# A two-group encoder layer: adaLN by channel quarters in column tiles, branch B's inverse rms through DRAM, the residual gate in the first head

## The chip, the cores and the metric

The kernel runs on one core of a Trainium2 chip. The metric is the time of one launch on the device, in microseconds. A NeuronCore has TensorE (PE: matmuls and transposes; PEld is its weight load), VectorE (DVE), ScalarE (ACT), GpSimd (POOL) and SyncE (SP). In this kernel every DMA is issued by SP, one after the other. Matmul operands lie in SBUF (128 partitions), results go to PSUM (8 banks of 2 KB in each partition), and inputs, outputs and some intermediate tiles lie in DRAM.

## What is computed

Two request groups of 1024 tokens and 1024 channels each ("prompt", then "sample") go through the same layer, in float32:

```python
shift, scale, gate = split(silu(c) @ w_ada + b_ada, 3)           # adaLN, per channel
h = rms_norm(x, norm_g) * (1 + scale) + shift
qa, ka, va, za, qb, kb, vb, zb, ga, gb = split(h @ w_in)         # 5376 columns
oa = gqa_attention(rope2d(rms(qa)), rope2d(rms(ka)), va) * silu(za)   # 8 q heads, 2 kv heads of 64
ob = diff_attention(rope(rms(qb)), rope(rms(kb)), vb, lam)            # 4 heads, two maps of 64 each
ob = rms_norm(ob, subln_g) * (1 - lam_init) * silu(zb)                # per head of 128
merged = sigmoid(ga) * (oa @ w_proj_a) + sigmoid(gb) * (ob @ w_proj_b)
y = x + gate * (merged @ w_out)
```

## The kernel before

**Number format.** Most operands are kept as two float32r tiles, a high part and a rest (`hh`, `hl` of the normalised input; `w[:, c, 0]`, `w[:, c, 1]` of a weight). A product is three matmuls, hh*wh, hh*wl and hl*wh, so 8 chunks of 128 channels give 24 matmuls for one output tile. The split costs a ScalarE copy and a VectorE subtraction (`split_w`). A matmul of plain float32 operands stands in the trace as two records.

**Layout.** `ht[hf][0][c]` is the high part of channels c*128.. of token half `hf`, 128x512, with channels on the partitions. `proj_tt` (L505) makes 128 tokens x 256 columns from it (k/v, q, qkb, vb); `z_gen` (L693) makes 128 columns x 512 tokens for the silu and sigmoid gates. A z output goes through the single buffer `ev` to a DRAM tile `zd`. One z weight load serves four outputs, in twelve steps.

**Order.** Each piece of work is a generator, and `weave` interleaves generators by written shares: a stream of n steps runs beside another of m steps with a lead given as a number. After that, the framework places instructions by a model of the machine's time, with the written order as priority; the order on every engine is then fixed in the program. `high_priority` puts attention steps 100 places forward.

**Stages of a group.** `head` (L1018): k/v of branch A (`kva_gen`), the first half of its queries (`qa_gen`) and z steps. `phase(0)` to `phase(4)`: attention of the halves of A and heads 0 to 2 of B as the main stream, beside the projections which the next phase needs and `Z_SHARE` (in outputs of three steps) z outputs. Last phase: attention of head 3, with `fill` (group 0: first `gate_gen`; then the remaining z steps and the first 16-TAIL merge steps of branch A) and `gates` (the gated outputs of heads up to B's 1). Then the TAIL merge steps that were held back, with the gated outputs of B's heads 2 and 3 (`then[1]`); branch B's merges; the output projection, with the next group's normalised input (`ht_gen`).

**The first head of group 0.** `start` (L337) loads w_ada in eight 1 MB pieces (512 rows x 512 columns) and multiplies each in `ada` (L294): the silu of c (`cT`, two columns, one for each group) is the stationary operand, so an output has 2 partitions x 512; `ada_end` (L300) copies it and turns it by four transposes into columns `modc`. Channels come in halves: shift and scale of channels 0 to 511 first. In between, x^T of the first 512 tokens is squared (ScalarE), added over chunks (`added`, four VectorE additions), summed over partitions by matmuls against a column of ones (`inv_rms`, L266, L271 its matmul), raised to -1/2 on GpSimd and spread over partitions (`spread`, L281). `modulated` applies scale and shift and splits. For the second 512 tokens `inv_rms` gets all 8 unsummed chunks: 4 x 8 matmuls. `start_late` normalises that half while the head already runs.

**gate_gen** (L445) makes the residual gate for both groups: 16 loads of 128 x 512, 16 matmuls of the same form as in `ada`, eight transposes.

**gated_gen** (L911) multiplies an attention output with its z and its inverse norm. Branch A's inverse sums of all heads are transposed at once, written to the DRAM row `rA` and read back, broadcast over partitions, into the two-buffer tile `tab`. Branch B's inverse rms (`ssB`) is spread by four transposes of a broadcast column for each output and half (L942), read from PSUM. `ssB` of a head is finished by GpSimd after its last attention unit (L868, L869).

**Buffers.** 15 tiles of 8 KB a partition (`utile`), two weight tiles, three `st` staging tiles, two `sbank` score tiles of two PSUM banks each, three `fbank` banks. While no attention runs (`alone`), `gbank` takes two of five from the score tiles.

## Time and profile before

| | us |
|---|---|
| median of 3 runs (1940.3 to 1945.74) | 1940.68 |
| the profiled execution | 1933.24 |
| its span, first to last instruction | 1931.5 |
| TensorE busy in the span | 1881.2 |
| VectorE / ScalarE / GpSimd busy | 1397.3 / 991.7 / 414.7 |
| group 0's head / first attention scores | ends at about 140 |
| group 1 begins | about 998 |

The page divides the span into 40 slices of 48 us; digits are tenths:

```profile
PE   8899999999999999999999999999989999999999
DVE  5669886778898677767465788688788767777731
DMA  9125465556554436875641455565545343477522
```

Page and views give, for a group of instructions, line, engine, operation, output<-input, shapes and count, then busy us and mean ns of one, then the idle time of the engine just before them and what ended it. Matmuls are pipelined, so the mean of one is longer than the spacing in a run of them. A view of stretches gives for each "from:to" its length and the busy us of PE, PEld, DVE, ACT and POOL, the granted TensorE clock, the DMA share and GB/s.

### The profile page before, as it was taken

How to read it: one execution, taken by the hardware profiler on the slowest of the kernel's cores; microseconds unless marked ns; L12 is line 12 of the kernel's file. 1: busy time of each engine (PE TensorE's matmuls, PEld its weight loads, DVE VectorE, ACT ScalarE, POOL GpSimd, SP SyncE). 2: the span in 40 equal slices, each digit the busy share in tenths (PEclk: the TensorE clock that was granted, in tenths of full speed). 3: DMA queues.
4: the chain of work that ended last, by engine and by line, in shares of the span. 5: the costliest groups of instructions: out<-in, count | busy, mean ns of one | idle time of the engine just before them, and what ended most of it. 6: DMA issues, size and time to landing. Idle time of an engine off the chain costs nothing.

```text
span 1931.5 us, 30797 instructions
## 1 busy us (share of the span) xinstructions
PE 1881.2 (97%) x10466; PEld 1610.0 (83%) x10466; DVE 1397.3 (72%) x2145; ACT 991.7 (51%) x2091; POOL 414.7 (21%) x758
## 2 busy tenths in 40 slices
PE   8899999999999999999999999999989999999999
PEld 3788888888988995778889888898877989888887
DVE  5669886778898677767465788688788767777731
ACT  4446665666666454414233566566666545542310
POOL 1342300120335051000124231013221524201000
PEclk9999999999999999999999999999999999999999
DMA  9125465556554436875641455565545343477522
GB/s 319 45 81 146 135 173 148 153 148 176 152 142 110 116 92 192 273 256 181 218 140 39 137 144 166 145 172 151 154 129 162 107 113 100 143 234 264 180 104 77
DMA packets 271613, 295.25 MB, mean 153 GB/s; under 512 B 37857, under 2 KB 220257, under 8 KB 271457
## 3 DMA queue, kind: packets, MB, share of 16 engines
q1 hardware_dynamic: 271456, 293.28, 51.4%
q8 instruction: 84, 1.38, 0.3%
q14 instruction: 73, 0.59, 0.1%
HBM read 133.72 MB, written 42.01 MB: 91 GB/s over the span
## 4 chain that ended last, share of the span: by engine, by line
PE 81%; DVE 7%; DMA 5%; issue 2%; ACT 2%; SPq 1%; POOL 1%; DVEq 0%; ACTq 0%; POOLq 0%
PE f L704 22%; PE f L515 19%; PE f L1007 5%; PE s L737 5%; PE a L839 5%; PE s L738 5%; PE f L976 4%; PE s L1007 4%; PE a L800 3%; PE a L799 3%; PE s L976 2%; DMA q<-p 2%; DVE m L739 2%; DVE p L774 1%; PE f L298 1%
## 5 line engine op out<-in xcount | busy, mean ns | idle before, releaser
L704 PE MATMUL f<-u,w 128*128 128x512 f32 x2232 | 574.2, 395 | 2.0 <-DVE ssB L863 1.5
L515 PE MATMUL f<-w,u 128*128 128x256 f32 x3456 | 487.5, 285 | 7.5 <-DVE u L571 3.7
L515 PEld LDWEIGHTS f<-w,u 128*128 128x128 f32 x3456 | 457.8, 190 | 29.0 <-DVE u L571 4.3
L704 PEld LDWEIGHTS f<-u,w 128*128 128x128 f32 x2232 | 404.2, 188 | 77.8 <-DVE ssB L863 1.8
L739 DVE TENSOR_REDUCE m<-s 128x1 f32<-128x1024 f32 x256 | 311.0, 1217 | 51.3 <-PE s L738 48.4
L774 DVE STREAM_TRANSPOSE p<-p 128x1024 f32<-128x1024 f32 x192 | 238.3, 1241 | 92.7 <-ACT p L741 89.3
L738 PE MATMUL s<-u,sw 128*128 128x512 f32 x512 | 203.8, 398 | 0.0
L788 DVE TENSOR_TENSOR q<-q,hi 128x512 fp32r<-128x512 f32 x256 | 171.5, 690 | 34.3 <-ACT hi L787 32.3
L787 ACT ACTIVATE hi<-q 128x512 fp32r<-128x512 f32 x256 | 153.6, 624 | 76.2 <-DMA q<-p 37.8
L741 ACT ACTIVATE p<-s,m,rsA 128x1024 f32<-128x1024 f32 x128 | 153.8, 1202 | 71.4 <-DMA q<-p 69.6
L178 ACT ACTIVATE w<-st 128x512 fp32r<-128x512 f32 x196 | 114.4, 625 | 99.2 <-DMA st<-in_w_in_dram 42.4
L741 ACT ACTIVATE p<-s,m,rsB 128x1024 f32<-128x1024 f32 x128 | 154.3, 1205 | 6.5 <-DMA q<-p 1.9
L179 DVE TENSOR_TENSOR w<-st,w 128x512 fp32r<-128x512 f32 x196 | 132.8, 706 | 34.2 <-ACT w L178 33.1
L658 POOL TENSOR_TENSOR row<-row,gB 128x96 f32<-128x96 f32 x64 | 33.8, 528 | 485.7 <-ACT row L529 474.1
L799 PE MATMUL a<-hi,u 128*128 128x256 f32 x512 | 132.2, 284 | 2.8 <-DMA q<-p 1.8
L800 PE MATMUL a<-q,u 128*128 128x256 f32 x512 | 129.3, 286 | 2.6 <-DVE q L788 2.6
L976 PE MATMUL f<-u,w 128*128 128x512 f32 x540 | 130.5, 393 | 1.3 <-DVE u L987 1.3
L839 PE MATMUL a<-q,u 128*128 128x256 f32 x512 | 127.1, 385 | 3.9 <-DVE oo L816 3.0
L976 PEld LDWEIGHTS f<-u,w 128*128 128x128 f32 x540 | 100.5, 188 | 23.0 <-DVE u L987 2.3
L839 PEld LDWEIGHTS a<-q,u 128*128 128x128 f32 x512 | 95.6, 193 | 20.0 <-DVE oo L816 3.6
L737 PE MATMUL s<-u 128*128 128x512 f32 x256 | 108.3, 424 | 3.3 <-ACT p L741 3.2
L737 PE MATMUL s<-u,u 128*128 128x512 f32 x256 | 102.4, 400 | 8.5 <-ACT p L741 3.1
(181 smaller groups left out, 2557.5 us busy)
## 6 DMA issues: line engine op xcount, KB each, us to landing
q<-p SPq DMA_DIRECT2D x768, 128.0 KB, 2.6
st<-in_w_in_dram SPq DMA_DIRECT2D x132, 256.0 KB, 3.1
zd<-ev SPq DMA_DIRECT2D x96, 256.0 KB, 2.2
sw<-u SPq DMA_DIRECT2D x256, 64.0 KB, 2.1
p<-zd SPq DMA_DIRECT2D x64, 256.0 KB, 3.7
u<-in_w_ada_dram SPq DMA_DIRECT2D x8, 1024.0 KB, 10.4
st<-in_w_in_dram SPq DMA_DIRECT2D x64, 128.0 KB, 2.8
st<-in_w_out_dram SPq DMA_DIRECT2D x32, 256.0 KB, 3.6
```

Source lines behind the costliest of these rows:

```text
L515: nc.tensor.matmul(ps, lt[c][:, sl], w[:, c, wi, :], start=(k == 0), stop=(k == 23))
L704: nc.tensor.matmul(ps, w[:, c, wi, e * P : (e + 1) * P], rt[c], start=(k == 0), stop=(k == 23),)
L737: nc.tensor.matmul(s[:, sl], q, k[:, sl], start=True, stop=False)
L738: nc.tensor.matmul(s[:, sl], sw, k[:, sl], start=False, stop=True)
L739: nc.vector.tensor_reduce(out=m, in_=s, axis=AX.X, op=ALU.max, negate=True)
L741: nc.scalar.activation(pt.rearrange("p (j c a) -> p j c a", j=4, c=8), s.rearrange("p (c a j) -> p j c a", c=8, j=4), AF.Exp, scale=rs, bi ...
L774: nc.vector.transpose(pt, pt)
L799: nc.tensor.matmul(acc, lt, th[:, c, :], start=(k == 0), stop=False)
L800: nc.tensor.matmul(acc, lt, tl[:, c, :], start=False, stop=(k == 7))
L839: nc.tensor.matmul(acc, u["v"][:, k], pT[:, k], start=(k == 0), stop=(k == 7))
L976: nc.tensor.matmul(ps, w[:, c, wi, d * P : (d + 1) * P], o[:, oi, :], start=(k == 0), stop=(k == 11))
L1007: nc.tensor.matmul(ps, w[:, c, wi, e * P : (e + 1) * P], m[:, mi, :], start=(k == 0), stop=(k == 23))
```

## The change

1. **adaLN by quarters.** `load_ada` loads, for a quarter of 256 channels, shift and scale side by side (two DMAs of 0.5 MB for each half of the rows). `ada` puts the four chunks of 128 input rows into four column tiles (output partitions 0, 32, 64, 96; `cpad` pads the stationary operand to 32 columns), so that the bank holds four partial sums; `ada_sum` adds and turns them by matmuls against `two`, a 128x2 matrix of ones at rows j*32+r.
2. **The first block.** SP now issues x first, then a quarter of w_ada, the k/v weight, the first z weight and the other quarters. After each quarter the first 512 tokens of these channels are scaled, modulated and split, and at once used: `kva_early` accumulates all four row tiles of k/v, `z_one` two z outputs, chunk by chunk, in banks held in `early`. `kva_gen` takes these as `given`. ScalarE, VectorE, TensorE and SP keep the written order there (`in_order`).
3. **z_first** finishes the first two z weights: two outputs for the first token half, then four at a time, chunk by chunk, for the second. Its second weight lies in two `utile`s.
4. `added` sums by running additions and is also used for the second token half, so `inv_rms` has 4 matmuls there.
5. **gate_gen** works by four quarters in column tiles and moves from group 0's last phase to its head, beside `qa_gen`.
6. **Branch B's inverse rms**: one transpose of `ssB` for two heads, a ScalarE copy and a write to a DRAM row `rB`; each output then reads its row, broadcast over 128 partitions, into `tab`.
7. **Written shares** differ, for each group: Z_SHARE, ATT_W, IN_A, Z_A, LAST_ATT, LAST_FILL, GATED_A, TAIL (5 for both groups; now 2 and 3) and TAIL_A. Group 0's head takes 35 z steps instead of 18, its last phase no gate steps.

```diff
-Z_SHARE = ((7, 19, 6, 3, 2, 4), (9, 14, 7, 3, 2, 6))
-Z_HEAD = (6, 5)
+Z_SHARE = ((8, 23, 6, 1, 1, 2), (13, 12, 7, 3, 0, 6))
+Z_HEAD = (8, 6)
 ...
-LAST_ATT = 44
-LAST_FILL = 26
-TAIL = 5
+LAST_ATT = (45, 45)
+LAST_FILL = (20, 24)
+TAIL = (2, 3)
+Z_FIRST = (22, 7)
 ...
+    def ada(wts, cpad):
+        acc = gbank()
+        for q, wt in enumerate(wts):
+            for c in range(4):
+                pe.matmul(
+                    acc[32 * c : 32 * c + 32], cpad[:, q * 4 + c], wt[:, c], start=(q == 0), stop=(q == 1),
+                    tile_position=(0, 32 * c),
+                )
+        part = rtile()
+        act.activation(part, acc, AF.Copy)
+        return part
+    def ada_sum(part):
+        ps = gbank()[:, :8].rearrange("p (t c g) -> p t c g", t=2, g=2)
+        for third in range(2):
+            for c in range(2):
+                o = third * 256 + c * P
+                pe.matmul(ps[:, third, c], part[:, o : o + P], two, start=True, stop=True)
+        return ps
 ...
     def start(ht):
+        xT = [load_xT0(0)]
+        wts = [load_ada(n) for n in range(2)]
+        kva_w.append(load_w(w_cols(w_in, (C_KA, 256)), early=True))
+        kva_w.append(load_w(w_cols(w_in, (C_ZA, 256)), early=True))
+        wts += [load_ada(n) for n in range(2, 8)]
+        rs = inv_rms(added(squares(xT[0])))
+        rsb = spread(rs)
+        early.update(kva=[x for b in two_banks() for x in (b[:, :256], b[:, 256:])], z=two_banks())
+        ps = ada_sum(ada(wts[:2], cpad))
+        for quarter in range(4):
+            cs = range(quarter * 2, quarter * 2 + 2)
+            by_rms(xT[0], cs, rsb)
+            split_early(kva_w[0][1], quarter)
+            ada_end(quarter, ps)
 ...
+            split_early(kva_w[1][1], quarter, act)
+            modulated(ht, 0, xT[0], cs)
+            split_early(kva_w[1][1], quarter, vec)
+            for c in cs:
+                kva_early(ht, c)
+            part = ada(wts[quarter * 2 + 2 : quarter * 2 + 4], cpad) if quarter < 3 else None
+            for c in cs:
+                for e in range(2):
+                    z_one(ht, 0, c, kva_w[1][0], e, early["z"][e], pe)
+                if part is not None:
+                    ps, part = ada_sum(part), None
+        xT.append(load_xT0(1))
+        kva_w.append((load_w(w_cols(w_in, (C_ZA + 256, 256)), room=(utile(), utile())),))
+        return lambda: start_late(ht, xT[1])
+    def start_late(ht, xT):
+        rsb = spread(inv_rms(added(squares(xT))))
 ...
     def gate_gen():
+        for n in range(4):
+            acc = gbank()[:, :256]
+            nc.vector.memset(acc, 0.0)
 ...
+                        nc.tensor.matmul(
+                            acc[32 * c : 32 * c + 2], cT[:, q * 4 + c], st[:, j], start=(q == 0), stop=(q == 1),
+                            tile_position=(0, 32 * c),
+                        )
 ...
     def gated_gen(st, i, hf, oT):
+        if i > 1 and hf == 0:
+            ss = st["ssB"][:, 2 * i - 4 : 2 * i - 2].rearrange("p j n -> p (j n)")
+            ps = fbank()[:16, :P]
+            nc.tensor.transpose(ps, ss, ident)
+            row = rtile()[:16, :P]
+            nc.scalar.activation(row, ps, AF.Copy)
+            dma(st["rB"][i - 2], row)
 ...
-                rb = gbank()
-                for k in range(4):
-                    r = st["ssB"][:, e - 4, hf * 4 + k : hf * 4 + k + 1]
-                    nc.tensor.transpose(rb[:, k * P : (k + 1) * P], r.to_broadcast([P, P]), ident)
+                dma(rb, rB[e % 2, hf].partition_broadcast(P))
 ...
     def head(g, st, zs, late):
         if g == 0:
-            for i in range(2):
-                weave((islice(kva, 6), 6, 0.0), (islice(zs, 3), 3, 0.0))
-                if i == 0:
-                    late()
-            weave((chain(kva, qa), 40, 0.0), (islice(zs, nz - 6), nz - 6, Z_HEAD_A[g]))
+            drain(islice(zs, 6))
+            late()
+            weave((kva, 27, 0.0), (islice(zs, Z_FIRST[0]), Z_FIRST[0], Z_FIRST_A[0]))
+            weave((qa, 27, 0.0), (islice(zs, Z_FIRST[1]), Z_FIRST[1], Z_FIRST_A[1]), (gate_gen(), 8, GATE_A))
 ...
         def fill():
-            if g == 0:
-                yield from gate_gen()
             yield from zs
             drain(first)
-            yield from islice(merge, 16 - TAIL)
+            yield from islice(merge, 16 - TAIL[g])
```

More of the change, by code (lines that the diff above doesn't have):

```diff
@@ L121, in gbank @@
         turn[0] += 1
-        if alone[0] and turn[0] % 5 in (0, 2):
+        if alone[0] and not early and turn[0] % 5 in (0, 2):
             return sbank()[:, :512]
@@ L205, in load_w @@
                 split_w(w, q, st)
-        return (w, sts) if early else w
+        cols = [w[c // 2][:, c % 2] for c in range(NCH)]
+        return (cols, (w, sts)) if early else cols
     def w_cols(mat, *cols):
@@ L317, in modulated, with by_rms @@
+    def by_rms(xT, cs, rsb):
+        for c in cs:
+            vec.tensor_tensor(out=xT[c], in0=xT[c], in1=rsb, op=ALU.mult)
     def modulated(ht, hf, xT, cs):
@@ L1106 @@
         load_tables_A(st)
-        zs = chain(*[z_item(st, i) for i in range(12)])
+        zs = chain(*([z_first(st)] if g == 0 else []), *[z_item(st, i) for i in range(0 if g else 2, 12)])
         head(g, st, zs, late)
```

310 lines of the change are left out of this document (174 added, 136 removed).

## The prediction

> **What bounds the kernel now.** I read the page's busy shares first, then busy times by stretch of the span, then the chain of work that ended last, then the matmul groups, and last the timeline of the first 60 us.
>
> ```profile
> PE 1881.2 (97%) x10466; PEld 1610.0 (83%) x10466; DVE 1397.3 (72%) x2145; ACT 991.7 (51%) x2091; POOL 414.7 (21%) x758
> ```
>
> TensorE is busy for 1881.2 of 1931.5 us, so two things can shorten the kernel: less TensorE work, or a part of the 50.3 us in which it idles. Where those lie is in the stretches (columns: busy us of TensorE, weight load, VectorE, ScalarE, GpSimd, each with its count; granted clock; DMA share; GB/s).
>
> ```profile
> 0.00:42.00 42.00, 34.29 (x103) 9.31 (x104) 19.85 (x36) 17.19 (x29) 5.36 (x10) 1.00 1.00 357
> 42.00:150.00 108.00, 98.58 (x639) 89.78 (x640) 71.85 (x183) 49.54 (x126) 36.50 (x58) 0.97 0.24 67
> 150.00:440.00 290.00, 285.54 (x1701) 252.56 (x1701) 232.80 (x314) 188.92 (x390) 53.75 (x90) 1.00 0.55 151
> 440.00:575.00 135.00, 133.93 (x786) 117.92 (x785) 113.14 (x166) 90.69 (x191) 36.13 (x72) 1.00 0.58 159
> 575.00:728.00 153.00, 153.00 (x953) 138.68 (x952) 113.44 (x168) 83.88 (x188) 62.58 (x130) 1.00 0.39 106
> 728.00:830.00 102.00, 95.93 (x402) 66.59 (x401) 75.20 (x108) 42.97 (x86) 8.50 (x21) 1.00 0.79 247
> ```
>
> In group 0, TensorE idles 7.7 us before 42 us, 9.4 in the rest of the head, 5.5 up to 575, none to 728 and 6.1 in the last attention phase. Before 42 us the DMA share is 1.00; there TensorE works, but mostly on adaLN:
>
> ```profile
> L298 PE MATMUL f<-u,cT 128*2 128x512 f32 x48 | 23.3, 642 | 6.8 <-DMA u<-in_w_ada_dram 6.8
> L298 PE MATMUL s<-u,cT 128*2 128x512 f32 x16 | 7.2, 592 | 0.0
> L452 PE MATMUL f<-st,cT 128*2 128x512 f32 x32 | 15.2, 592 | 1.2 <-DMA st<-in_w_ada_dram 1.2
> ...
> 29.68 10.39 PE f L298 x24
> 45.35 7.18 PE f L271 x50
> ...
> 140.91 5.47 PE f L704 x24
> 842.83 0.44 PE f L942 x4
> 998.23 8.63 PE f L515 x72
> ```
>
> The lower rows are of the chain (start, length, what, count) and give what one record costs in a run of them: adaLN 10.39/24 = 0.433 us, sum of squares (L271) 0.144, gate and z matmuls (L704) 0.228, projection by rows (L515) 0.120, four transposes of an inverse rms (L942) 0.44. An fp32 matmul leaves two records: 32 in the adaLN loop give 48+16.
>
> **The terms of the sum**, against the profiled execution's own 1933.24 us (span 1931.5 and 1.7 around it).
>
> *adaLN in column tiles (ada).* Before: 23.3+7.2 = 30.5 us. After: the same 64 records, but four neighbours write to different quarters of the output partitions. No row shows column tiles. If all four run at once, 16 rounds of 0.433 = 6.9 us is one end; one after the other, 30.5 is the other. The rows speak for the low end: a record with a 2-column weight costs 0.433 us for 512 moved rows, so columns of the array lie unused. I add 1.7 because the first 16 records took 9.21 us (below) against 6.9 at 0.433, and 0.45 for each of four blocks to enter and leave the mode (twice 0.592-0.433, a record's length less its spacing, and some gap): 10.4. Term: -20.1 (ends -23.6 and 0).
>
> *gate_gen.* Before, 32 x 0.433 = 13.9 us of the last phase. After, 64 records of half the length: 13.9 in turn, 3.5 four at once; with 8 entries of 0.16 I take 4.8. Term -9.1 (ends -10.4, +2.6). Its 16 loads go from the phase with a DMA share of 0.79 to the one with 0.24; on SP they now stand among qa's weight loads, and the three st buffers are shared, so each pair waits for the matmuls of an earlier one. That is hidden as long as the 25 us of qa's matmuls (192 x 0.120 = 23) last.
>
> *two, ada_sum.* The four partial rows are summed by 24 matmuls against `two`, 48 records at 0.144 = 6.9 us, for 24 transposes at 0.1 (row below) = 2.4. Term +4.5. The copy of a whole bank on ScalarE is followed by z matmuls ahead of the sums in the written order, which hide it; else it costs 0.6 a quarter.
>
> *added in start_late.* The second half's squares are added on VectorE first: 64 records become 8. 56 x 0.144 = 8.1. Term -8.1. The four additions (1.2 us each, as L260 to L262) run on VectorE while TensorE is in the first block, where VectorE has 5.5 us of work a quarter against 9 on TensorE (both below); uncovered they would cost 4.4.
>
> *rB.* Sixteen groups of four transposes (0.44) fall away, four single ones stay: 7.0 - 0.4. Term -6.6. Each broadcast becomes a 256 KB load, 2 MB per group of requests; group 0's last phase loses 4 MB of gate weights, group 1's loses nothing.
>
> *The front.* The first block (four row tiles of k/v and two z tiles) now starts after x, one quarter of adaLN and rms:
>
> ```profile
> 13.36 2.40 ACT L254 ACTIVATE q<-u 128x512 f32<-128x512 f32 x4 [0.22 <-DMA u<-in_xT_prompt_dram]
> 16.93 0.38 PE L307 MATMUL f<-ident,p 2*128 2x2 f32 x4 [0.86 <-DVE p L304]
> 19.21 0.69 DVE L263 TENSOR_TENSOR q<-q 128x512 f32<-128x512 f32 x1
> 20.75 1.05 PE L271 MATMUL f<-ones_c,q 128*128 128x1 f32 x8
> 22.38 1.03 POOL L278 TENSOR_TENSOR rs<-ss,nhalf 128x4 f32<-128x4 f32 x1
> 28.70 0.65 PE L285 MATMUL s<-ident,rs 128*128 128x128 f32 x4
> 29.38 0.60 ACT L287 ACTIVATE ev<-s 128x512 f32<-128x512 f32 x1 [3.71 <-PE s L285]
> ...
> 6.85 9.21 PE L298 MATMUL f<-u,cT 128*2 128x512 f32 x16 [6.85 <-DMA u<-in_w_ada_dram]
> L323 DVE TENSOR_SCALAR u<-u,modc 128x512 f32<-128x512 f32 x2 | 1.0, 536 | 0.0
> L327 DVE TENSOR_TENSOR u<-u,u 128x512 fp32r<-128x512 f32 x4 | 2.5, 672 | 0.0
> DMA packets 628, 1.22 MB, mean 407 GB/s; under 512 B 32, under 2 KB 32, under 8 KB 628
> DMA packets 400, 0.38 MB, mean 383 GB/s; under 512 B 26, under 2 KB 400, under 8 KB 400
> ```
>
> From the last square (15.76) to the pow (23.41) there are 7.7 us, then 0.9 to TensorE, 0.65 and 0.7: 9.9 to a ready rsb, without the wait for adaLN matmuls. With x first in SP's queue its 2.1 MB are in at about 8.5 us and the squares done at 9.7; the additions now overlap more, so rsb is there at about 19. Scaling by rms, weight split, modc and one chunk (0.54 and 0.67) on VectorE come to 3.6 us: first k/v matmul at about 22.6; a whole quarter is 5.5 us on VectorE. Until then TensorE has 6.8 us of work, so it idles 15.8, against 7.7 before: +8.1. Afterwards a quarter gives 24 x 0.120 + 12 x 0.228 = 5.6 us, with adaLN and sums 9: more than its 2.1 MB at 383 GB/s (5.5; the last two rows are 3 us of 2 KB packets and 1 us of 1 KB packets), so I let TensorE bound the block, to 55 us. On SP the tables and the second half of x come behind all this, in written order, and nothing in the block reads them. Term +8.1 (ends +3, if rms comes 5 us earlier, and +16, if VectorE or DMA paces it).
>
> *Rest of the head.* It gets z_first's chunkwise second half and 17 more z steps as filling; 9.4 us idle should shrink. Term -4 (ends -9, and +5 because both score banks are held by z_first until a single ev buffer has let four outputs pass).
>
> *Z work leaves the late phases of group 0.* A z output takes three steps, Z_SHARE counts in threes. Steps are 35 in the head, 24, 69 and 18 in the first three phases: all 144 are gone, so that phases 3, 4 and the last have none. Ten z outputs (240 x 0.228 = 54.7 us) and the gate (13.9) leave 575 to 830; three merge steps (12 x 0.228) come. TensorE: 248.9 - 68.6 + 8.2 = 188.5. VectorE: 188.6, less 10 x 0.69, 8 weight splits of 0.69, 1.7 for the gate, plus 2.1 = 176.6. If TensorE alone bound it, the stretch would shrink with its work; but VectorE would have to be busy for 94%. The densest stretches above reach 0.80 (150 to 440) and 0.84 (440 to 575) with TensorE nearly full. I take 0.87, as VectorE is now close to being the bound: 203 us, against 188.5+6.1 = 194.6. Term +8 (ends -6 and +44, at the 0.74 that it has now).
>
> *The tail round trip.* Heads 2 and 3 now need, after the last pow, a transpose, a copy, a write and a broadcast read:
>
> ```profile
> rA<-row SPq DMA_DIRECT2D x2, 32.0 KB, 2.3
> tab<-rA SPq DMA_DIRECT2D x32, 128.0 KB, 3.8
> ...
> 849.36 1.97 POOL L869 TENSOR_TENSOR ssB<-ssB,nhalf 128x8 f32<-128x8 f32 x1
> ```
>
> 2.3+3.8, two issues of 0.5, 0.3 and 0.4 are 7.8 us more than a transpose straight from ssB. TAIL leaves 2 and 3 merge steps of 2.7 us, and the first halves of branch B's merges need only heads 0 and 1. I take 2 us of stall per group: +4 (ends 0 and +15.6). Queued on SP behind a write that waits for pow are branch B's weights and gate tiles, for which the merges wait next.
>
> Sum: -20.1 - 9.1 + 4.5 - 8.1 - 6.6 + 8.1 - 4 + 8 + 4 = -23.3, hence 1909.9 for a profiled execution. The median shown, 1940.68, lies 7.4 above the profiled one; with the same offset **1917 us**. Group 1's own weights (ATT_W, IN_A, TAIL) are retimed too; it idles 12.3 us in 1400 to 1500, the worst of it here, and I give that nothing, with 6 either way:
>
> ```profile
> 1400.00:1425.00 25.00, 19.19 (x105) 15.56 (x105) 20.86 (x29) 16.40 (x35) 7.02 (x14) 0.92 0.60 163
> ```
>
> **Two rules beside the rows.**
>
> ```profile
> 45.00:52.00 7.00, 7.00 (x52) 7.00 (x51) 5.00 (x16) 2.56 (x5) 0.00 (x0) 0.77 0.35 85
> 52.00:54.00 2.00, 2.00 (x7) 1.71 (x8) 1.15 (x4) 0.72 (x2) 1.10 (x2) 0.50 0.66 224
> 52.53 3.69 PE s L704 x9
> ```
>
> After 7 us of one-column matmuls the granted clock was 0.50, and nine z matmuls took 0.41 us instead of 0.228: 1.6 us, which go with the 56 records. A new dip at the first k/v matmuls I price the same, so the two cancel. The Trainium skill (TensorE: Matmul & The Clock Gate, Part 1) says that a window of some 3.4 us without enough work halves the clock for the next one; the 0.50 agrees. By it each quarter that waits could start slow, an estimate of four times 1.7 us, and the sum would give 1922.
>
> The other rule speaks against the tiles: the Trainium skill (TensorEngine Tiling (Array Packing), Key Properties) has a change of tiling mode drain the array. No run here shows it; my 0.45 and 0.16 above come from rows, and with twice as much for each entry the sum would be 1920.
>
> **Rivals.**
> 1. *VectorE keeps group 0's late phases* (chance 0.13). It stays at 0.74 of the time, its share in both late rows now: 176.6/0.74 = 239 us instead of 203, 1917+36 = 1953, slower. At 0.83 VectorE goes with 5.8 us of TensorE idle in the row of 1400; against it, 0.84 with a full TensorE in 440 to 575. It decides from 0.78 down (226 us, no gain left).
> 2. *Column tiles run in turn* (0.09). adaLN stays at 30.5 and the gate at 13.9+2.6: 1917+20+12 = 1949, less some of the front's idle, 1945: no change to slightly slower. For it: no row shows any overlap of two matmuls' moved rows.
> 3. *The round trip isn't covered* (0.08): both tails stall for 7.8, 1917+11.6 = 1929.
> 4. *The idle also goes* (0.20): half of group 1's 12.3, the front at +3 and the late stretch at 0.93 (190): 1917-6-5-13 = 1893.
>
> **Numbers.** My forecast has 0.50 and its own range is 1902 to 1930. The range 1892 to 1947 reaches to rivals 2, 3 and 4 and leaves out most of the first. A measurement of this kernel tells about 0.3% (5.8 us) from nothing: faster is 0.50+0.20+0.08 and a little of rivals 1 and 2, 0.80; same 0.07; slower, most of rivals 1 and 2, 0.13.
>
> **What would show it.** In the changed profile: adaLN records four deep, 64 in about 10 us, not 30; first k/v matmul at 21 to 24 us; one group of 8 sum-of-squares records in the second half; TensorE's total near 1842; from the last z matmul to the end of group 0's attention a VectorE share of 0.85 to 0.9 and some 14 us of TensorE idle. It is wrong if that share stays at 0.75, if the front idles over 24 us, or if the merges after either attention wait over 5 us for `tab`.

## The result and the profile after

The changed kernel takes 1956.76 us (median of 4 runs, 1954.99 to 1960.12) beside 1941.57 for the kernel before in the same measurement: a ratio of 1.0077, 95% interval 1.0055 to 1.0098. It is slower by some 15 us; 1917 was forecast. The profiled span grew from 1931.5 to 1956.1 us. First the page's row of busy times, after:

```profile
PE 1876.7 (96%) x10406; PEld 1614.5 (83%) x10406; DVE 1396.2 (71%) x2174; ACT 985.1 (50%) x2087; POOL 400.5 (20%) x756
```

TensorE's 1881.2 us became 1876.7, not 1842. But its busy time is also time at a lower clock. The two views of stretches that follow are cut at the same events in both kernels: first score matmul, first and last value matmul of branch B, first output matmul, for group 0 and then group 1 (columns as in the front part). Before:

```profile
0.00:139.00 139.00, 121.87 (x688) 89.89 (x689) 83.19 (x209) 61.52 (x144) 41.86 (x68) 0.98 0.45 150
139.00:554.00 415.00, 409.79 (x2417) 361.48 (x2415) 334.61 (x456) 269.61 (x557) 84.55 (x149) 1.00 0.55 152
554.00:830.00 276.00, 269.61 (x1475) 223.47 (x1476) 208.48 (x306) 142.06 (x307) 76.40 (x161) 1.00 0.55 162
830.00:910.00 80.00, 80.00 (x370) 66.32 (x369) 57.31 (x92) 21.00 (x35) 2.49 (x2) 1.00 0.60 203
...
1074.00:1485.00 411.00, 396.75 (x2345) 349.29 (x2343) 333.65 (x463) 266.95 (x560) 85.75 (x155) 0.99 0.55 152
1485.00:1770.00 285.00, 282.00 (x1559) 246.67 (x1559) 211.18 (x301) 143.97 (x306) 75.76 (x155) 0.99 0.53 156
```

After:

```profile
0.00:172.00 172.00, 150.52 (x891) 120.60 (x891) 96.10 (x241) 61.60 (x140) 35.59 (x64) 0.98 0.50 154
172.00:608.00 436.00, 431.36 (x2498) 378.01 (x2498) 341.17 (x481) 278.89 (x583) 85.72 (x160) 0.99 0.59 155
608.00:882.00 274.00, 247.99 (x1330) 211.77 (x1329) 208.88 (x304) 132.09 (x284) 72.94 (x154) 0.93 0.56 152
882.00:934.00 52.00, 48.47 (x201) 38.82 (x200) 39.30 (x66) 17.15 (x29) 1.85 (x2) 0.93 0.72 224
934.00:1022.00 88.00, 88.00 (x395) 72.97 (x394) 46.18 (x67) 26.45 (x48) 12.78 (x10) 1.00 0.58 196
...
1106.00:1518.00 412.00, 405.71 (x2392) 356.76 (x2391) 336.74 (x464) 270.42 (x566) 83.62 (x156) 1.00 0.59 152
1518.00:1798.00 280.00, 266.77 (x1468) 231.57 (x1467) 208.64 (x304) 138.87 (x299) 72.84 (x154) 0.98 0.57 161
```

Four things stand there. Group 0 ends at 1022 instead of 998 us: the whole loss lies in it, as group 1 takes 934 us both times. The head is 33 us longer, since z work and the gate came into it. Branch B's attention (third row) takes 274 us instead of 276 although it has 145 TensorE records fewer; TensorE idles 26.0 us there, not 6.4, and the granted clock is 0.93, not 1.00. VectorE's share is 208.88/274 = 0.76, as before (208.48/276 = 0.76).

So I split each span into three parts, summed over stretches of 20 us: *work* (busy time times granted clock, what TensorE would need at full clock), *clock loss* (busy time times one minus clock) and *idle*.

| | span | work | clock loss | idle |
|---|---|---|---|---|
| before | 1931.5 | 1872.4 | 8.7 | 50.3 |
| after | 1956.1 | 1846.6 | 30.1 | 79.4 |
| difference | +24.6 | -25.8 | +21.4 | +29.1 |

The change does spare TensorE work. In these two executions it is all given back, and nearly as much again, as idle and as slow clock. (The one before lies 8.3 us below its kernel's median and the one after 1.2 above, so some 9 of the 24.6 us are the choice of execution; the medians differ by 15.2.) In branch B's attention of group 0 alone the idle grew by 19.6 us and the clock loss by about 0.07 x 248 = 17 us: 37 of the 50.

The stretch behind that attention (fourth row) fell from 80 to 52 us, because 168 matmul records of branch A's merges, not 40, now stand ahead of the attention's end. Over both rows some 74 us of TensorE work at full clock left, but only 30 us of time: 44 came back, 23 as idle and 21 as clock loss.

The z matmuls show what left that stage. Before, in 554 to 830 us, and after, in 590 to 640 us (count, duration in ns, first and last start):

```profile
L704 PE MATMUL f<-u,w x240: 387/389/582, 575.8 to 812.3; 128*128 128x512 f32 x120
```

```profile
L816 PE MATMUL f<-u,w x54: 387/390/477, 589.9 to 607.1; 128*128 128x512 f32 x54
```

Before, 240 z matmuls are spread up to 812 us. After, the last one starts at 607; what is left to put between the attention steps are projections and then merges, and merges need gated outputs. Where the idle is (after, by stretch):

```profile
750.00:775.00 25.00, 18.26 (x66) 13.34 (x65) 23.84 (x36) 16.15 (x37) 8.83 (x19) 0.75 0.62 177
775.00:800.00 25.00, 16.52 (x57) 11.29 (x56) 16.12 (x23) 6.63 (x13) 1.54 (x4) 0.84 0.80 237
800.00:825.00 25.00, 23.29 (x79) 17.89 (x79) 18.58 (x27) 8.07 (x18) 1.19 (x2) 0.73 0.77 214
```

The chain of waits for 775 to 806 us, after (start, length, what; L1051 multiplies an attention output by its z, L1060 splits the result, L845 is the maximum of a score tile):

```profile
784.36 4.19 DMA row<-zd
...
788.58 0.70 DVE row L1051
...
789.30 3.20 DMA row<-zd
...
792.59 0.70 DVE row L1051
...
793.31 3.32 DMA row<-zd
...
799.84 3.97 DMA tab<-rA
...
804.39 1.22 DVE m L845
```

The gated products of six outputs come one behind the other: a load of 3 to 4 us into one of three `row` buffers, 0.70 us of VectorE, which frees a buffer for the next load. Score maxima of the attention stand behind them in VectorE's queue (L845 at 804.39). The waits of VectorE in 608 to 882 us, after, put it at

```profile
DVE row L1051 <- DMA row<-zd: 8.5, 6, 3.0
```

8.5 us in 6 waits, beside 5.0 in 4 for the same wait before; two other waits of VectorE in this stage come to more (10.7 us for ScalarE, 10.3 for TensorE). VectorE is busy for only 16.12 and 18.58 of 25 us in the two last of those stretches: there it is late, not full. In the first of them, with 23.84 of 25, it is nearly full.

The front, in the timeline of TensorE, after (start, length, what, count; L99 is the helper that keeps the written order):

```profile
24.39 0.80 PE L99 MATMUL s<-w,u 128*128 128x256 f32 x2 [1.30 <-ACT u L99]
25.70 5.06 PE L99 MATMUL s<-w,u 128*128 128x256 f32 x22 [0.51 <-DVE u L99]
30.69 2.51 PE L99 MATMUL f<-u,at 128*32 128x512 f32 x16
...
38.19 2.90 PE L99 MATMUL s<-w,u 128*128 128x256 f32 x22 [0.81 <-DVE u L99]
41.01 1.92 PE L99 MATMUL f<-u,at 128*32 128x512 f32 x16
```

The first k/v matmul starts at 24.39 us, and 16 column-tile records take 1.92 us, 0.12 each beside 0.433 for one in the loop before. The fourth quarter comes behind the sums of squares of the second half; its 22 k/v records start at 61.58 us and take 4.87, and the granted clock falls (a line of the timeline, then two stretches):

```profile
59.88 1.84 PE L302 MATMUL f<-ones_c,q 128*128 128x1 f32 x8 [1.57 <-DVE q L294]
...
58.00:64.00 6.00, 4.42 (x21) 4.25 (x21) 5.30 (x11) 2.12 (x4) 0.00 (x0) 0.60 0.34 98
64.00:70.00 6.00, 6.00 (x32) 5.37 (x31) 0.91 (x4) 0.78 (x2) 1.21 (x2) 0.83 0.29 91
```

The block's last z matmul ends at 69.2 us. The groups of lines, after:

```profile
L99 PE MATMUL s<-w,u 128*128 128x256 f32 x96 | 17.9, 353 | 4.7 <-ACT u L99 2.5 <-DVE u L99 2.1
...
L99 PE MATMUL f<-u,at 128*32 128x512 f32 x64 | 10.0, 754 | 0.0
L524 PE MATMUL s<-st,cT 128*2 128x256 f32 x48 | 5.7, 378 | 0.0
L99 PE MATMUL f<-two,row 128*128 128x2 f32 x32 | 4.7, 269 | 0.7 <-ACT row L99 0.7
L302 PE MATMUL f<-ones_c,q 128*128 128x1 f32 x16 | 3.7, 353 | 13.9 <-DVE q L294 13.9
```

### The profile page after: what moved, and what is told of

The parts are those of the page before. It is cut to its first block, busy times and chain, and to the rows that moved or that the text cites. A ratio compares the mean times of both kernels' runs of the same rounds, so it can differ in the third digit from the quotient of the medians.

```text
span 1956.1 us, 30770 instructions
## 1 busy us (share of the span) xinstructions
PE 1876.7 (96%) x10406; PEld 1614.5 (83%) x10406; DVE 1396.2 (71%) x2174; ACT 985.1 (50%) x2087; POOL 400.5 (20%) x756
## 4 chain that ended last, share of the span: by engine, by line
PE 71%; DVE 10%; DMA 8%; SPq 4%; ACT 3%; issue 3%; POOL 0%; ACTq 0%; DVEq 0%; POOLq 0%
PE f L592 18%; PE f L816 15%; PE f L1118 6%; PE f L1087 5%; PE s L843 4%; PE a L945 4%; PE s L844 4%; PE s L1118 3%; DMA q<-p 3%; SPq L885 3%; DVE m L845 2%; PE a L906 2%; PE a L905 2%; PE s L1087 2%; DVE q L894 1%
## 5 line engine op out<-in xcount | busy, mean ns | idle before, releaser
L816 PE MATMUL f<-u,w 128*128 128x512 f32 x1992 | 513.9, 396 | 2.7 <-DVE w L198 1.1
L592 PE MATMUL f<-w,u 128*128 128x256 f32 x3360 | 467.3, 285 | 1.8 <-ACT ev L773 1.1
L592 PEld LDWEIGHTS f<-w,u 128*128 128x128 f32 x3360 | 440.5, 191 | 23.0 <-issue 2.2
L816 PEld LDWEIGHTS f<-u,w 128*128 128x128 f32 x1992 | 363.2, 190 | 71.8 <-DVE w L198 1.7
L845 DVE TENSOR_REDUCE m<-s 128x1 f32<-128x1024 f32 x256 | 311.0, 1216 | 24.6 <-PE s L844 21.7
L894 DVE TENSOR_TENSOR q<-q,hi 128x512 fp32r<-128x512 f32 x256 | 171.4, 690 | 42.8 <-ACT hi L893 39.8
L847 ACT ACTIVATE p<-s,m,rsB 128x1024 f32<-128x1024 f32 x128 | 154.2, 1205 | 26.3 <-DMA q<-p 11.5
L197 ACT ACTIVATE w<-st 128x512 fp32r<-128x512 f32 x188 | 109.5, 625 | 93.7 <-DMA st<-in_w_in_dram 35.8
L1087 PE MATMUL f<-u,w 128*128 128x512 f32 x588 | 150.1, 409 | 4.7 <-DVE u L1060 2.8
L198 DVE TENSOR_TENSOR w<-st,w 128x512 fp32r<-128x512 f32 x188 | 127.1, 708 | 30.0 <-ACT w L197 29.3
L1087 PEld LDWEIGHTS f<-u,w 128*128 128x128 f32 x588 | 115.1, 198 | 32.4 <-DVE u L1060 4.5
L843 PE MATMUL s<-u 128*128 128x512 f32 x256 | 111.2, 435 | 20.3 <-ACT p L847 20.1
L736 POOL TENSOR_TENSOR row<-row,gB 128x96 f32<-128x96 f32 x64 | 30.3, 473 | 472.0 <-ACT row L606 472.0
L844 PEld LDWEIGHTS s<-u,sw 128*128 128x128 f32 x512 | 98.6, 193 | 15.7
```

The source lines that it names most:

```text
L592: nc.tensor.matmul(ps, lt[c][:, sl], w[c][:, wi, :], start=(k == 0), stop=(k == 23))
L816: nc.tensor.matmul(ps, w[c][:, wi, e * P : (e + 1) * P], rt[c], start=(k == 0), stop=(k == 23),)
L843: nc.tensor.matmul(s[:, sl], q, k[:, sl], start=True, stop=False)
L844: nc.tensor.matmul(s[:, sl], sw, k[:, sl], start=False, stop=True)
L845: nc.vector.tensor_reduce(out=m, in_=s, axis=AX.X, op=ALU.max, negate=True)
L847: nc.scalar.activation(pt.rearrange("p (j c a) -> p j c a", j=4, c=8), s.rearrange("p (c a j) -> p j c a", c=8, j=4), AF.Exp, scale=rs, bi ...
```

## The experiments

Five theories stood. **Theory 1**: z work placed early leaves group 0's last attention without filling (rival 1 of the prediction). **Theory 2**: the gated products and their loads, now given a lead of 0.1 instead of -0.3 (GATED_A), hold up VectorE's queue there. **Theory 3**: a single part costs it, above all the round trip `rB`, or the gate's new place, or branch B's tables, which are now loaded behind the head. **Theory 4**: the new written shares are at fault by themselves. **Theory 5**, formed after the first eight runs: the order on every engine is fixed by a model, the old shares fit the old code, and any edit loses that fit. "Idle" below is TensorE's in group 0, cut as above; ratios are to the kernel before, with 95% intervals.

### Z work alone (theories 1 and 2)

e1: the changed kernel with group 0's z work late; e2: the kernel before with its z work early.

```diff
-    (8, 23, 6, 1, 1, 2),        # e1, Z_SHARE of group 0
-LAST_FILL = (20, 24)
-Z_FIRST = (22, 7)
+    (6, 18, 6, 3, 2, 2),
+LAST_FILL = (29, 24)
+Z_FIRST = (18, 0)
```

```diff
-    (7, 19, 6, 3, 2, 4),        # e2, Z_SHARE of group 0
-Z_HEAD = (6, 5)
+    (8, 23, 6, 1, 1, 2),
+Z_HEAD = (12, 5)
```

> The changed kernel with group 0's z steps moved back towards its late phases: 24 in the head instead of 35, then 18, 54, 18, 9 and 6, and 15 left for the last phase. Theory 1 (group 0's late phases lost their filling matmuls, so VectorE and the latencies of attention show as TensorE idle): TensorE's idle between 613 and 890 us falls by 20 us or more, time 1920 to 1935. Rival 2 (gated outputs, which GATED_A now puts first, block VectorE's queue while their loads are under way): the stall stays in the last phase, time 1945 to 1957. Rival 3 (branch B's round trip through DRAM stalls the tails): no change, 1950 to 1960.

> The kernel before with only group 0's z steps moved early (36 in the head, then 24, 69, and the rest in the third phase), all else as it was. Theory 1: slower by 15 to 30 us than before, 1955 to 1970, with TensorE idle appearing after the last z matmul. Rivals 2 and 3: within 6 us of before, 1935 to 1947.

e2 takes 1983.87 us, 1.0216 (1.0185 to 1.0246), more than theory 1 expected. Its attention of A, then of B:

```profile
175.00:612.00 437.00, 428.02 (x2488) 376.64 (x2488) 332.67 (x457) 273.88 (x570) 85.23 (x150) 1.00 0.54 150
612.00:908.00 296.00, 257.79 (x1368) 210.56 (x1366) 213.87 (x316) 133.26 (x288) 76.28 (x160) 0.93 0.53 154
```

No other part of the change is in it, and B's attention idles 38.2 us at a clock of 0.93, the picture of the changed kernel. The idle there comes from z work that was moved away; GATED_A is still -0.3 in it, so theory 2 isn't needed for it. What e2 shows is this place of the idle; its time by itself says little, as edits that move no work cost as much (theory 5, below). e1, in which GATED_A is 0.1 as in the changed kernel, takes 1962.78, 1.0107 (1.0075 to 1.0138), the same rows:

```profile
153.00:590.00 437.00, 406.93 (x2326) 355.44 (x2326) 341.69 (x484) 272.17 (x569) 84.28 (x156) 0.95 0.57 148
590.00:890.00 300.00, 290.31 (x1568) 251.77 (x1569) 215.50 (x312) 142.62 (x304) 72.59 (x154) 0.98 0.55 156
```

Most of B's idle is gone (9.7 us are left), and A's attention now idles 30.1. The place of the idle follows the z work; its amount doesn't shrink, and the 1920 to 1935 us that theory 1 expected did not come.

### How much of it (theory 1, by amount)

e17 and e18, the last two to run, leave 16 and 13 of 144 z steps to the last phases of the changed kernel.

```diff
-    (8, 23, 6, 1, 1, 2),        # changed kernel
-LAST_FILL = (20, 24)
+    (8, 17, 6, 1, 1, 2),        # e17
+LAST_FILL = (30, 24)
+    (8, 20, 4, 1, 1, 2),        # e18
+LAST_FILL = (27, 24)
```

> The changed kernel with 18 fewer z steps in phase 1 of group 0: 6 go to phases 3 and 4, some 10 (3.3 outputs, 80 matmul records, 18 us of TensorE) to the last phase. If the idle there follows the z work that is left: B attention's idle falls from 26 to 12-19 us, the granted clock there rises from 0.93 to 0.95 or more, A attention's idle rises from 5 to 10-20, and the time is 1945 to 1962. If late loads alone make the idle: B keeps 24 us or more.

> As e17 with 9 fewer steps in phase 1 and 6 fewer in phase 2: 6 steps in phases 3 and 4, some 7 in the last phase. B attention's idle 14 to 22 us if it follows the z work left, A attention's 5 to 15; 1945 to 1962. B keeps 24 us or more if late loads alone make it.

e17 takes 1959.45, 1.0093 (1.0077 to 1.0108), e18 1962.80, 1.0114 (1.0088 to 1.0140). e17's attention of A and B:

```profile
174.00:596.00 422.00, 403.01 (x2325) 351.18 (x2324) 333.42 (x471) 270.35 (x565) 83.06 (x158) 0.98 0.58 150
596.00:886.00 290.00, 272.90 (x1498) 236.65 (x1497) 216.04 (x314) 141.20 (x302) 68.04 (x154) 0.98 0.57 160
```

B's idle runs 26.0 (after), 22.8 (e18), 17.1 (e17), 9.7 (e1); A's, in the same order, 4.6, 15.0, 19.0, 30.1. The sum is 30.6, 37.8, 36.1 and 39.8. e17 is as theory 1 expected in idle, clock and time; e18 lies 0.8 us above the upper ends, in B's idle and in time. None of the amounts beats the changed kernel, let alone the one before.

The same dependence runs through all twenty kernels of this document, those below included, when the z matmul records (L704 before, L816 after, or the same line in the run's own kernel) of each stage are counted:

| stage | z records in it | kernels | idle there |
|---|---|---|---|
| B | 0 to 26 | after, e2, e3, e4, e8, e9, e13, e14 | 26.0 to 38.2 |
| B | 144 and 165 | e18, e17 | 22.8 and 17.1 |
| B | 240 to 264 | before, e1, e5 to e7, e10 to e12, e15, e16 | 6.4 to 15.7 |
| A | 810 to 864 | after, e2, e3, e4, e8, e9, e13, e14 | 3.3 to 10.0 |
| A | 696 to 720 | e1, e5, e6, e17, e18 | 15.0 to 30.1 |
| A | 768 to 792 | before, e7, e12 | 4.5 to 7.6 |
| A | 768 to 792 | e10, e11, e15, e16 | 18.5 to 20.4 |

The last two rows have the same z work and not the same idle, so in A something else counts too: theory 5, below.

### Single parts (theory 3)

e3: the changed kernel with the four transposes of the kernel before in place of `rB`. e4: `gate_gen`, column tiles and all, back in the last phase. e7: the kernel before with only `rB` added (the reverse of e3). e9: the tables' loads left to the scheduler's order.

```diff
-            weave((qa, 27, 0.0), (islice(zs, Z_FIRST[1]), Z_FIRST[1], Z_FIRST_A[1]), (gate_gen(), 8, GATE_A))
+            weave((qa, 27, 0.0), (islice(zs, Z_FIRST[1]), Z_FIRST[1], Z_FIRST_A[1]))   # e4
+            if g == 0:
+                yield from gate_gen()                                                  # e4, first in fill()
-            dma_next(gB[:, i, :], t[src][0].partition_broadcast(P))
+            dma(gB[:, i, :], t[src][0].partition_broadcast(P))                         # e9, and three more
```

> The changed kernel with branch B's inverse rms spread by four transposes for each output again, no row in DRAM. Rival 3: the idle at both attentions' ends (8.7 us in 850 to 900, 9.1 in 1725 to 1800) falls by 10 or more, TensorE gets 6.6 us of work back, time 1945 to 1952. Theory 1 and rival 2: the tails idle for other reasons, the transposes cost what they did, 1957 to 1965.

> The changed kernel with gate_gen (in its new form, by quarters in column tiles) back in group 0's last phase. Theory 1: its matmuls, some 5 us, and its copies lie in a stretch that idles anyway, and the head loses them: 3 to 8 us faster, 1948 to 1954. Rival 2: its loads queue between the gated outputs' loads on SP, same or slower, 1955 to 1965.

> The kernel before with branch B's inverse rms through DRAM alone. By the prediction -6.6 of TensorE work and +4 of stall: 1934 to 1940. Rival 3: tails stall by 7.8 each, 1943 to 1955.

> The changed kernel, with only the loads of branch B's tables given back to the scheduler's order (they stood at 161-174 us, behind the rest of the head's loads, on the chain of waits). If the late tables cost what that stretch shows, the first attention of branch A begins 6 to 10 us earlier (head 172 -> 163 to 166 us) and the time is 1946 to 1951. If the loss is z work taken from group 0's late phases, TensorE still idles 24 to 28 us in group 0's B attention, and the time is 1953 to 1958. If any change of order moves the stalls about, stages whose code is untouched (group 1) change by more than 5 us.

| | us | ratio | idle A, B | clock in B |
|---|---|---|---|---|
| after | 1956.76 | 1.0077 (1.0055 to 1.0098) | 4.6, 26.0 | 0.93 |
| e3 no rB | 1970.85 | 1.0142 (1.0111 to 1.0174) | 3.3, 30.8 | 0.91 |
| e4 gate last | 1965.01 | 1.0121 (1.0087 to 1.0155) | 10.0, 34.4 | 0.93 |
| e9 tables free | 1971.17 | 1.0155 (1.0119 to 1.0190) | 4.4, 33.1 | 0.92 |
| e7 before + rB | 1950.33 | 1.0054 (1.0039 to 1.0069) | 4.5, 7.5 | 0.99 |

None of the three parts, taken out of the changed kernel, makes it faster, and B keeps its idle each time; e9's head even took 179 us instead of 172, where 163 to 166 were expected. Theory 1's times missed as well (1948 to 1954 for e4, 1957 to 1965 for e3). The idle is what decides here, as a difference of 10 us in time says little once theory 5 (below) is known. In e7 the round trip spares 6.5 us of TensorE work (1872.4 to 1865.9) and group 0 ends only 2 us later; the rest of its loss is in group 1's head and attention, whose written code before the gated outputs is untouched. Its time lies in the range of rival 3, but the stretches behind the two attentions, where that rival puts the stall, idle only 0.2 and 2.1 us. That pointed to theory 5.

### The shares (theory 4)

e5: the changed code with the old shares and weights (group 0's z shares as in e1). e6: e5 with the gate in the last phase and without `rB`, so that the new front is nearly all that is left. e8: the old code with the new shares and weights.

```diff
-ATT_W = (
-    (0.944, 1.073, 1.232, 1.085, 1.038, 1.663),
+    (1.07, 0.933, 1.1, 0.95, 1.129, 1.52),      # e5, e6; likewise Z_SHARE, IN_A, Z_A, LAST_*, GATED_A, TAIL, TAIL_A
```

> The changed kernel's code with the shares of before (ATT_W, IN_A, Z_A, LAST_ATT, GATED_A, TAIL, TAIL_A, group 1's z shares; group 0's z late as in the first experiment, LAST_FILL 26). Theory 4 (the new shares, not the new code, cost the time): TensorE's idle in group 0's attention falls back to about 12 us, time 1910 to 1930. Theory 1 (what counts is only that the z steps are early): as the first experiment, 1950 to 1965. Rival 3 (round trip): 1950 to 1960, with idle in the tails.

> Only the new first head: as the run with the shares of before, and besides gate_gen (new form) in the last phase and branch B's transposes again. If the front alone is worth what the prediction gave it (adaLN -20.1, sums of squares -8.1, the gate's tiles -9.1, sums +4.5, idle +8.1): 1912 to 1922. If the new block's idle takes it back: 1935 to 1945.

> The kernel before with the new shares (z early as in the second experiment, and the new ATT_W, IN_A, Z_A, LAST_ATT 45, GATED_A, TAIL 3, TAIL_A, group 1's z shares). Theory 1: the z steps decide, 1975 to 1995 as in the second experiment. If the new weights were fitted to the early z steps: 1945 to 1965.

| code | old shares | new shares |
|---|---|---|
| before | 1941.57 | e8: 1978.02 (1.0202, 1.0174 to 1.0229) |
| changed | e5: 1993.85 (1.0285, 1.0253 to 1.0318) | 1956.76 |

e6 takes 1988.98 (1.0251, 1.0225 to 1.0278). Each code is fast with its own shares and some 37 us slower with the other's. Theory 4 finds no support: with the old shares the changed code is slower, not faster. But edits that change no work cost as much as these 37 us (below), so it isn't shown that the new shares by themselves save them. e5 and e6 lie above every range that was expected; e8 lies in theory 1's, with 4.0 us of idle in A and 30.4 in B.

### Edits that change no work (theory 5)

e10, e15: the kernel before with the counter that spreads tiles over the two kinds of PSUM banks beginning at 1 and at 2. e13, e14: the same in the changed kernel. e11: one z output of the kernel before moved from the second phase to the first.

```diff
-    turn = [0]
+    turn = [1]                  # e10, e13; [2] in e15, e14
-    (7, 19, 6, 3, 2, 4),
+    (8, 18, 6, 3, 2, 4),        # e11
```

> The kernel before with no work changed: only the counter that spreads tiles over two kinds of PSUM bank begins at 1 rather than 0. If the order on the engines is a fit to the exact code, so that any edit costs stalls, this alone costs 8 to 40 us (1950 to 1980). If stalls come from where work is put (z work, the round trip), it stays within 3 us of before.

> The kernel before with one z output tile more in phase 0 and one fewer in phase 1 (24 of some 8000 matmuls move by one phase; the late phases keep theirs). By the theory of the starved late phases: no change, within 3 us. By the theory that the order is a fit to exact numbers: 8 to 40 us slower, with the loss spread over stages that the edit doesn't touch.

> The changed kernel, no work changed, the PSUM counter begins at 1. If the changed kernel's order is fitted as closely to its code as the old one's was (26 to 46 us below its neighbours): 1978 to 2003. If it is an ordinary order: within 8 us of 1957, to either side. Group 0's B attention keeps 24 us or more of TensorE idle in both cases, as that comes from the moved z work.

> As e13 with the counter at 2: 1978 to 2003 if the changed kernel is fitted as closely as the old one, within 8 us of 1957 if not. Group 0's B attention idles 24 us or more.

> The kernel before, no work changed, the counter begins at 2. If its order is a fit that any edit loses: 1960 to 1990, as the other neighbours (1965, 1985). If e10 was one bad order among mostly good ones: 1938 to 1948. Group 0's B attention idles under 12 us.

| | us | ratio | work | clock loss + idle | idle A, B |
|---|---|---|---|---|---|
| before | 1941.57 | 1 | 1872.4 | 59.0 | 5.2, 6.4 |
| e10 before, counter 1 | 1984.80 | 1.0231 (1.0199 to 1.0262) | 1873.6 | 107.5 | 18.5, 8.9 |
| e15 before, counter 2 | 1972.53 | 1.0163 (1.0139 to 1.0187) | 1877.5 | 90.4 | 18.9, 8.6 |
| e11 before, one z | 1965.27 | 1.0122 (1.0087 to 1.0158) | 1875.2 | 90.4 | 20.4, 7.3 |
| after | 1956.76 | 1.0077 (1.0055 to 1.0098) | 1846.6 | 109.5 | 4.6, 26.0 |
| e13 after, counter 1 | 1995.53 | 1.0286 (1.0254 to 1.0318) | 1846.1 | 147.3 | 8.0, 30.3 |
| e14 after, counter 2 | 1998.61 | 1.0301 (1.0275 to 1.0326) | 1841.9 | 153.1 | 4.0, 35.7 |

A counter that begins at another value costs the kernel before 32 and 45 us, and one z output 24. TensorE's work stays within some 5 us in each of the two kernels' families; what changes is idle and clock. e10 lies above the range that was expected for a fit, the four others within theirs. In e10 the stage of group 0 that loses most is one in which the edit moves nothing, branch A's attention (the rows of A and B):

```profile
150.00:582.00 432.00, 413.54 (x2389) 361.69 (x2387) 333.68 (x460) 270.49 (x559) 80.57 (x156) 0.98 0.53 147
582.00:863.00 281.00, 272.05 (x1478) 226.23 (x1478) 208.59 (x305) 140.54 (x304) 72.36 (x154) 0.99 0.55 159
```

The changed kernel loses just as much by the same edits, 41 and 43 us, which is what an order that fits its code as closely would do. e13, the same rows:

```profile
186.00:624.00 438.00, 429.97 (x2486) 375.93 (x2487) 342.94 (x479) 279.24 (x579) 86.92 (x157) 1.00 0.58 152
624.00:904.00 280.00, 249.65 (x1336) 212.48 (x1335) 206.30 (x302) 132.40 (x284) 72.51 (x153) 0.93 0.55 152
```

In it the loss lies elsewhere: A's attention is only 2 us longer than in the changed kernel, but the head 14 (186 instead of 172) and group 1 17 (951 instead of 934).

So theory 5 holds for what an edit costs, but alone it doesn't make the 15 us. (The counter also decides which tiles share a bank outside of attention, so it is not an order alone; inside attention it decides nothing. The loss of e13's head may be of that kind.) Compared at the same counter, by difference of ratios, the change costs 0.0077 (counter 0), 0.0055 (counter 1) and 0.0138 (counter 2), 11 to 27 us, fit or no fit. And B's idle tells the two families apart in every pair: 6 to 9 us in the old one, 26 to 36 in the changed one.

### Savings without moved work

e12: the kernel before with `added` for the second half and the gate in column tiles, left in the last phase. e16: the same at counter 1.

```diff
-        rs = inv_rms([q[:, c] for q in squares(xT[1]) for c in range(4)])
+        rs = inv_rms(added(squares(xT[1])))
...
+                        nc.tensor.matmul(
+                            acc[32 * c : 32 * c + 2], cT[:, q * 4 + c], st[:, j], start=(q == 0), stop=(q == 1),
+                            tile_position=(0, 32 * c),
+                        )
```

> The kernel before with the two TensorE savings that need no filling moved: the squares of the second half added up before the ones matmul (32 records fewer -> 8, -8 us) and the gate in four column tiles, left in the last phase (-9 us). If TensorE's work is what the time follows wherever its order stays near that of before: 1922 to 1930. If late phases of group 0 need all of their TensorE work as filling, the gate's 9 us turn into idle there (gate is in the last phase): 1932 to 1936. If any edit reshuffles the order at a price: 1940 to 1965.

> e12's savings with the counter at 1. If what TensorE is spared shows once both sides have lost the fit: 10 to 20 us under e10's 1985 (1965 to 1975). If the spared work turns to idle, or order alone decides: anywhere from 1950 to 2000 with no tie to e10.

e12 takes 1957.99, 1.0095 (1.0059 to 1.0131), though its TensorE work fell by 8.4 us to 1864.0. e16 takes 1979.09, 1.0194 (1.0167 to 1.0221), beside e10's 1.0231: some 7 us less, where 10 to 20 were expected, with 8.3 us less work (1865.3 to 1873.6). That would be a gain of about the size of the spared work against a kernel whose order has lost its fit as well, but the two intervals overlap, so it isn't shown. Against the kernel before, e12 lies in the range expected for a new order at a price. My forecast of 17 us for these two (8.1 and 9.1), 15.7 with the gate's third of the new sums, was about twice what they spared.

## Why the prediction was wrong

**The step that failed** is *Z work leaves the late phases of group 0*, a term of +8 with VectorE taken at 0.87. From the last z matmul to the end of that attention its share was 0.76 (208.88 of 274 us), and the stage lost 37 us more than before as idle and clock, within the bound of +44 that the prediction gave and far from the value taken. The reason for 0.87 was "VectorE is now close to being the bound". The runs showed otherwise: VectorE's share was 0.76 before and after and 0.72 to 0.74 in e1, e2 and e17, whatever TensorE had to do. Nor did its work fall by the 12 us that the step counted: it was 208.48, then 208.88 us. And not three merge steps (36 records) came into the stage, but 128 records, out of the stretch behind it. With that stretch, the idle and the lost clock came to 44 us, where the prediction had +8 here and +2 for group 0's tail.

The stage's length follows TensorE's work only in part: from the changed kernel to e17 and e1 the work in it is 231, 267 and 285 us at full clock, the length 274, 290 and 300. So about half of the work taken out between these becomes idle or clock loss. Rival 1, with 0.13, had this: VectorE kept at about its share, 1953, "decides from 0.78 down". Its price for the stage was about right, 44 us against 37; that its time lies only 4 us from the measured one is partly luck, as it holds no clock loss and all 39.4 us of TensorE savings, of which 25.8 came. And that VectorE itself sets the pace is only part of it: it is nearly full from 750 to 775 us, but behind that the chain shows loads of `zd` and `rA` between its instructions. Whether a fourth `row` buffer would shorten that was not tried.

**The second miss is inside the TensorE terms.** Together they came to -20.1 - 9.1 + 4.5 - 8.1 - 6.6 = -39.4; the work at full clock fell by 25.8.
- adaLN was right: 30.5 to 10.0 us of records, forecast 10.4. Rival 2 (tiles in turn) is refuted.
- The sums against `two`: 4.7 us in the front and 1.6 + 0.6 in the gate, forecast 6.9 together.
- The gate: 5.7 + 1.8 = 7.5, forecast 4.8. `added`: 10.2 to 3.7 for both halves, -6.5 instead of -8.1.
- `rB`: -6.5 in e7, forecast -6.6.
- Missing from the sum: the first block's k/v matmuls took 17.9 us, not 96 x 0.120 = 11.5, as the first quarter's 22 (5.06 us) and the fourth's (4.87) ran at little more than half the pace of the two between (2.90 each). The fourth's slowness is clock loss (0.52 granted from 61.58 to 66.20 us), so of the 13.6 missing some 4 are k/v, and some 2 more the block's z matmuls (12.8 us against 48 x 0.228). About 7 are the gate and `added` together, as e12 shows them: 8.4 spared instead of 15.7. These are estimates; about 1 us isn't assigned.

The two misses, 44 - 10 = 34 and 13.6 us, make nearly all of the 47.9 between the forecast of -23.3 and the +24.6 of the profiled executions.

**The front** was right in size: the first k/v matmul at 24.39 us (21 to 24 forecast), and the head's idle 21.5 us against 17.1: +4.4, for which +8.1 - 4 stood. But the block ended at 69 instead of 55. Of the two rules beside the rows, the first came in part: two of the four quarters ran slow, by 2.2 and 2.0 us, where an estimate of four times 1.7 stood. For the second, no price shows: behind the 16 tiled records that start at 41.01 us and take 1.92, the next matmul starts at 42.87.

**The tail** was covered as forecast: TensorE idles 3.5 us between group 0's last attention and the output projection (at a clock of 0.93), 0.5 in group 1; +4 was the term. Rival 3 isn't needed. **Group 1** took the same time as before, as assumed; its idle only moved, from 14.2 to 6.3 us in A's attention and from 3.0 to 13.2 in B's. Rival 4 (the idle also goes) is the opposite of what happened.

**What no term of the sum held**: clock loss. The sum priced idle at its own length. Behind the idle of 750 to 825 us the granted clock is 0.73 to 0.84, and over the kernel the clock loss grew by 21.4 us, nearly as much as the idle (29.1).

**And what stood behind all terms**: that the rest of the kernel stays as it is. Edits with no work in them, or one z output of 48, cost 24 to 45 us. Both kernels lie that far below such neighbours, so between the two the price may cancel, but it is as large as the whole forecast. What is shown, then, is that the idle in group 0's late phases comes from the z work that left them. That it alone makes the 15 us isn't: in e1, e17 and e18, with z work moved back, the idle goes to A's attention and no time is won. Open are also which instruction of a new order is late first, and what e12 would take with shares of its own.

## What to carry to other kernels

Where attention is woven with independent matmuls, those matmuls can be what keeps TensorE from idling, as in the late phases here (26 to 38 us of idle without them, 6 to 16 with them); before moving them forward, look how far the stage's length follows TensorE's work, and price each idle microsecond with the clock behind it. Where the order of all engines comes from a model and written shares, compare a change not only with the kernel before, but with neighbours of it that differ by an edit without work: here that alone was 32 to 45 us, two to three times the effect in question. A split of the span into work at full clock, clock loss and idle shows what a saving spared even where the order hides it.

## What the runs showed of the hardware

Idle costs more than its length here: 29.1 us more of idle came with 21.4 us of clock loss. In the other runs, all but e7, each microsecond of idle beyond the kernel before came with 0.3 to 0.9 us of clock loss, and attention stages with 26 to 38 us of idle ran at 0.91 to 0.96 of the clock. The Trainium skill (TensorE: Matmul & The Clock Gate, Part 1) says that the default state is throttled and that activity releases it; the trace agrees, with 0.73 to 0.84 around the gaps of 750 to 825 us.

The recorded clock doesn't show every slow start. In the first quarter of the block 22 k/v records filled 4.90 us at a recorded clock of 1.00, in the second 2.80 (stretches of the kernel after). In the fourth, at nearly the pace of the first, the clock is recorded as 0.60 (58 to 64 us, above):

```profile
25.70:30.60 4.90, 4.90 (x22) 4.76 (x22) 2.90 (x5) 0.00 (x0) 0.00 (x0) 1.00 1.09 348
38.20:41.00 2.80, 2.80 (x22) 2.68 (x22) 2.77 (x5) 0.00 (x0) 0.00 (x0) 1.00 1.15 229
```

What slowed the first quarter isn't shown; the spacing shows it, and the clock column doesn't. And four column tiles of plain float32 matmuls, 32 columns each, ran at 0.12 us a record in the last two groups of 16 (the first two took 3.64 and 2.51 us), where one in the loop before takes 0.433: 3.6 times as fast.
